# First MLP layer by seven block products instead of eight, and remainders formed by accumulating DMA

## The chip, the cores and the metric

The kernel runs on one core of a Trainium2 chip. The metric is device time in microseconds, and the time of a kernel is the median of its runs. A core has TensorE (matmuls, called PE in the profile; its weight loads are PEld), VectorE (DVE), ScalarE (ACT), GpSimd (POOL) and SyncE (SP, which issues the loads here). They run beside each other and wait for one another through semaphores. Matmuls read operands from on-chip memory and add into accumulation banks (PSUM); transfers between memories are DMAs.

## The reference

One decoder block on 512 tokens of width 1024, in float32: a gated token mixer (convolution and attention branches), and then the MLP, which is what the change touches:

```
h = rms_norm(x, g_pre_mlp) * (1 + scale2) + shift2        # 512 x 1024
y = square(relu(h @ w_mlp_in)) @ w_mlp_out                # 1024 x 4096, 4096 x 1024
x = x + gate2 * rms_norm(y, g_post_mlp)
```

## The kernel before

**Three-pass products.** TensorE multiplies in a rounded 32-bit format. To keep float32's accuracy every operand v is held as two parts, a rounded h and a remainder l = v - h, and a product is three matmuls, h·h, h·l and l·h (`mm3`, line 452). `split` (line 457) makes the parts of a block: ScalarE copies it into the rounded format, VectorE subtracts that from the original. `W` (line 470) does the same for a unit of weights, which is 128 partitions x 1024 words here; `wunit` (line 490) loads one by a 512 KB DMA on SP's queue and splits it.

**Memory.** Float data live in one arena (`f_arena`, 22400 words a partition), rounded data in another (`r_arena`, 28000 words), accumulators in eight banks. `Arena.alloc` (line 87) gives out places in program order; a buffer's place can be that of an earlier one, whose last reader is then waited for.

**Order of the work.** Every operation is recorded first (`Planner`, line 167). The planner then runs through them with a table of costs: TensorE takes its instructions in the order of the program (`key`, line 325), each other engine the ready one with the earliest due time; a DMA is ready when its buffer is free. The places are chosen again up to eight times (`PASSES`, line 47) with the times of the plan before, and the shortest plan is issued (line 385). So all instructions of the profile bear line 388, and groups are told apart by tile and shape.

**The MLP.** After normalization, transposes bring the tokens' features onto the partitions; `h2` (line 1345) holds them as 8 pairs of 128 x 512 (feature block k, all tokens), filled in two halves of 256 tokens. The 4096 hidden features are worked through in `NCH` = 4 chunks of `HPC` = 8 tiles of 128 (lines 1361 and 1362). Per chunk:

- *First layer* (from line 1526): tiles in groups of `GRP`, four at once for the first group of chunk 0 (in two halves of 256 tokens, as these come in), two at once later. Each tile is 8 feature blocks x 3 matmuls of 512 columns into a bank; ScalarE then does relu and square into `hid`.
- *Second layer* (`strassen`, line 1442): the chunk's 512 x 1024 by 1024 x 1024 product as a 2 x 2 block product with seven block products instead of eight (Strassen's scheme in Winograd's order). Sums and differences of blocks are made by VectorE on the float data and then split; `b_form` (line 1457) splits the weight blocks, two units a product, `a_form` (line 1452) the activations. A product is 2 x 4 x 3 matmuls of 512 columns. `banked` (line 1555) adds the banks to the running output and, in the last chunk, finishes the row norms and stores.

Between the layers of different chunks there is no dependence other than through buffers; `h2` stays in the rounded arena until the last chunk's first layer (line 1546).

Of the kernel before, what the change touches and what calls it, by code (L numbers as in the profile page):

```python
# [17 lines left out]
P = 128  # L18
# [374 lines left out]
def tile_hybrid_block(  # L393
# [46 lines left out]
    def emit(past, replay):  # L440
# [904 lines left out]
        h2 = []  # L1345

        def yl(t, k):
            return ra.v(mT[k][0])[:, t * P:(t + 1) * P], ra.v(mT[k][1])[:, t * P:(t + 1) * P]
# [15 lines left out]
        def hid_weights(n0, n, i0=0):  # L1364

            return {(i, kh): wunit(w_mlp_in, 4 * kh, (n0 + i) * P, 4, 256) for i in range(i0, n, 2) for kh in range(2)}

        ws0 = {(0, 0): wunit(w_mlp_in, 0, 0, 4, 256)}
        for tp in range(2):
# [25 lines left out]
            if tp == 1:  # L1395
# [4 lines left out]
            if tp == 0:  # L1400
                h2[:] = [pair(T) for _ in range(KD)]
            hsl = slice(tp * 256, (tp + 1) * 256)
            for k2 in range(KD // 2):
                b = pb.alloc()
                for q in range(2):
                    for t in range(2):
                        k = 2 * k2 + q
                        pe.transpose(pb.v(b)[:, (2 * q + t) * P:(2 * q + t + 1) * P], fa.v(xn[t])[:, k * P:(k + 1) * P], ident)
                for q in range(2):
                    k = 2 * k2 + q  # L1410
                    ps, v = pb.v(b)[:, q * 256:(q + 1) * 256], fa.alloc(256)
                    hb, lb = h2[k]
                    if k == 0:
                        act.activation(ra.v(hb)[:, hsl], ps, AF.Identity, scale=mod[:, 3, k:k + 1], bias=mod[:, 2, k:k + 1])
                        dve.tensor_scalar(fa.v(v), ps, mod[:, 3, k:k + 1], mod[:, 2, k:k + 1], ALU.mult, ALU.add)
                    else:
                        act.activation(fa.v(v), ps, AF.Identity, scale=mod[:, 3, k:k + 1], bias=mod[:, 2, k:k + 1])
                        act.copy(ra.v(hb)[:, hsl], fa.v(v))
                    dve.tensor_tensor(ra.v(lb)[:, hsl], fa.v(v), rf(hb)[:, hsl], ALU.subtract)
                    fa.free(v)  # L1420
                pb.free(b)
            fa.free(*xn)
        fa.free(G1)


        def h2s(k, a, n):
            return tuple(ra.v(b)[:, a:a + n] for b in h2[k])

        ysb = []
        G2, fin = None, []  # L1430
# [11 lines left out]
        def strassen(hv, block, banked):  # L1442
# [76 lines left out]
            banked(1, 0, ba)  # L1519
            pb.free(*ba)  # L1520

        for ch in range(NCH):
            hid = fa.alloc(HPC * T)
            hv = fa.v(hid, "p (k t) -> p k t", k=HPC)
            GRP = 4 if ch == 0 else 2
            for n0 in range(0, HPC, GRP):
                bs = [pb.alloc() for _ in range(GRP)]
                ws = ws0 if ch == 0 and n0 == 0 else hid_weights(ch * HPC + n0, GRP)
                step = 256 if ch == 0 and n0 == 0 else T
                for t0 in range(0, T, step):  # L1530
                    for i in range(GRP):
                        for k in range(KD):
                            mm3(pb.v(bs[i])[:, t0:t0 + step], ws[i - i % 2, k // 4](k % 4, (i % 2) * P, P), h2s(k, t0, step),
                                k == 0, k == KD - 1)
                for w in ws.values():
                    w.free()
                for i in range(GRP):
                    r = fa.alloc(T)
                    act.activation(fa.v(r), pb.v(bs[i]), AF.Relu)
                    act.activation(hv[:, n0 + i], fa.v(r), AF.Square)  # L1540
                    fa.free(r)
                    pb.free(bs[i])
                if ch >= NCH - 2:
                    take(late, ADAS[1])
            if ch == NCH - 1:
                for p_ in h2:
# [87 lines left out]
```

## Time and profile before

| | us |
|---|---|
| median of 3 runs | 838.59 (838.47 to 839.24) |
| profiled execution, its own time | 836.4 |
| its span, first to last instruction | 834.6 |
| TensorE busy | 808.1 |
| VectorE busy | 685.2 |
| ScalarE busy | 415.5 |
| POOL busy | 45.4 |
| DMA moved | 117.28 MB, 141 GB/s over the span |

All durations and stages come from the profiled execution. Its own time is 2.2 us below the median, and its span another 1.8 us below that. A matmul's record is longer than the distance to the next one, because matmuls overlap; a busy TensorE therefore means an occupied one, and the pace is read from starts. Idle time of an engine is given with what ended it; idle time of an engine that does not bound costs nothing.

### The profile page before, as it was taken

Reading aid. Unit: us, or ns where it says so; the run is one execution under the profiler, and the core shown is the slowest. Engines: PE = TensorE matmul, PEld = TensorE weight load, DVE = VectorE, ACT = ScalarE, POOL = GpSimd, SP = SyncE. Lnnn points to the kernel's source line nnn. Section 1 sums busy time; section 2 is a strip of 40 time slices with the busy share of each in tenths; the row PEclk is TensorE's granted clock in tenths of the full one; section 3 lists DMA queues with packets and bytes.
Section 4 is the critical chain, followed back from the end, with each engine's and each line's share of the span. In section 5 each row is a group of like instructions: output and inputs, shape, how many; then the busy total and the mean of one; then the engine's idle time right before and its main releaser. Section 6 shows DMA issues by size and latency. Waiting matters only on the chain.

```text
span 834.6 us, 10659 instructions
## 1 busy us (share of the span) xinstructions
PE 808.1 (97%) x3940; PEld 675.7 (81%) x3940; DVE 685.2 (82%) x1012; ACT 415.5 (50%) x680; POOL 45.4 (5%) x119
## 2 busy tenths in 40 slices
PE   6999999999999989999999989999999999999995
PEld 3777888899988868888888779888888888888884
DVE  4979979999999997999999779298529993975696
ACT  5463363375893346227434287375346544553641
POOL 3001040000000020000000230000000000000002
PEclk9999999999999999999999989999999999999998
DMA  9997423202353141332799650064014831660302
GB/s 310 336 311 234 148 69 98 67 27 77 101 177 102 51 128 49 101 111 91 233 353 363 210 201 27 26 202 152 0 51 132 290 132 51 197 206 1 101 1 101
DMA packets 86823, 117.28 MB, mean 141 GB/s; under 512 B 7274, under 2 KB 60627, under 8 KB 86770
## 3 DMA queue, kind: packets, MB, share of 16 engines
q1 hardware_dynamic: 86770, 116.59, 43.5%
q8 instruction: 31, 0.51, 0.2%
q14 instruction: 22, 0.18, 0.1%
HBM read 108.18 MB, written 8.39 MB: 140 GB/s over the span
## 4 chain that ended last, share of the span: by engine, by line
PE 85%; DMA 4%; DVE 3%; POOL 2%; issue 2%; ACT 2%; SPq 1%; DVEq 0%; POOLq 0%; ACTq 0%
PE psum L388 85%; DMA f_arena<-in_w_in_dram 4%; DVE f_arena L388 3%; SPq L388 1%; POOL stats L388 1%; ACT f_arena L388 1%; DMA f_arena<-in_x_dram 1%; ACT r_arena L388 1%; POOL lns L388 1%; DVE r_arena L388 0%; DVEq L1629 0%; POOLq L1629 0%; DMA rows<-in_kv_norm_g_dram 0%; DVE mod L388 0%; DVE cols L388 0%
## 5 line engine op out<-in xcount | busy, mean ns | idle before, releaser
L388 PE MATMUL psum<-r_arena 128*128 128x512 f32 (+2 forms) x3592 | 766.5, 374 | 4.0 <-ACT r_arena L388 2.5
L388 PEld LDWEIGHTS psum<-r_arena 128*128 128x128 f32 x3592 | 634.4, 190 | 121.0 <-ACT r_arena L388 3.6
L388 DVE TENSOR_TENSOR r_arena<-f_arena,r_arena 128x1024 fp32r<-128x1024 f32 (+4 forms) x232 | 247.9, 1090 | 97.1 <-PE psum L388 48.5
L388 ACT CAST r_arena<-f_arena 128x1024 fp32r<-128x1024 f32 (+4 forms) x222 | 209.7, 966 | 183.3 <-PE psum L388 111.5
L388 DVE SCALAR_TENSOR_TENSOR f_arena<-f_arena,cw 128x512 f32<-128x512 f32 x240 | 164.8, 743 | 0.0
L388 ACT ACTIVATE f_arena<-psum 128x512 f32<-128x512 f32 x64 | 38.0, 597 | 119.6 <-PE psum L388 111.3
L388 DVE TENSOR_TENSOR f_arena<-f_arena 128x1024 f32<-128x1024 f32 (+3 forms) x78 | 77.0, 1003 | 8.3 <-ACT f_arena L388 6.3
L388 ACT ACTIVATE f_arena<-f_arena 128x512 f32<-128x512 f32 (+3 forms) x100 | 58.5, 604 | 20.2 <-DVE f_arena L388 19.4
L388 DVE SCALAR_TENSOR_TENSOR f_arena<-f_arena,cT 128x256 f32<-128x256 f32 (+2 forms) x84 | 55.2, 699 | 0.1
L388 PE MATMUL psum<-ident,f_arena 128*128 128x128 f32 (+1 forms) x240 | 35.3, 288 | 11.7 <-DVE f_arena L388 7.7
L388 PEld LDWEIGHTS psum<-ident,f_arena 128*128 128x128 f32 (+1 forms) x240 | 29.2, 148 | 17.2 <-DVE f_arena L388 8.7
L388 POOL TENSOR_SCALAR stats<-stats 128x1 f32<-128x1 f32 x32 | 14.8, 463 | 467.0 <-ACT r_arena L388 361.6
L388 DVE TENSOR_TENSOR f_arena<-psum,f_arena 128x512 f32<-128x512 f32 x52 | 35.2, 684 | 4.2 <-PE psum L388 3.9
L388 ACT CAST r_arena<-psum 128x512 fp32r<-128x512 f32 (+2 forms) x57 | 30.2, 566 | 15.8 <-PE psum L388 15.4
L388 DVE TENSOR_TENSOR r_arena<-psum,r_arena 128x512 fp32r<-128x512 f32 (+2 forms) x57 | 35.7, 656 | 2.2 <-ACT r_arena L388 1.9
L388 ACT COPY f_arena<-psum 128x512 f32<-128x512 f32 (+4 forms) x42 | 19.9, 500 | 23.0 <-PE psum L388 22.7
L388 ACT ACTIVATE r_arena<-f_arena 128x512 fp32r<-128x512 f32 (+3 forms) x20 | 13.0, 648 | 21.9 <-DVE f_arena L388 18.8
L388 DVE CUSTOM_DVE_ANT_0 f_arena<-psum,mask 128x128 f32<-128x128 f32 (+3 forms) x32 | 15.0, 484 | 2.5 <-PE psum L388 2.5
L388 POOL TENSOR_SCALAR lns<-lns 128x1 f32<-128x1 f32 x4 | 5.3, 1326 | 198.5 <-ACT r_arena L388 198.5
L388 POOL TENSOR_TENSOR stats<-stats,nhalf 128x1 f32<-128x1 f32 x24 | 15.2, 633 | 1.9
L388 DVE TENSOR_SCALAR f_arena<-f_arena,stats 128x1024 f32<-128x1024 f32 x8 | 6.0, 754 | 9.9 <-POOL stats L388 9.7
L388 DVE SCALAR_TENSOR_TENSOR f_arena<-f_arena 128x512 f32<-128x512 f32 (+1 forms) x18 | 13.1, 742 | 0.0
(93 smaller groups left out, 195.4 us busy)
## 6 DMA issues: line engine op xcount, KB each, us to landing
f_arena<-in_w_ada_dram SPq DMA_DIRECT2D x16, 1024.0 KB, 5.6
f_arena<-in_w_mlp_in_dram SPq DMA_DIRECT2D x32, 512.0 KB, 5.1
f_arena<-in_w_mlp_out_dram SPq DMA_DIRECT2D x32, 512.0 KB, 5.2
f_arena<-in_w_in_dram SPq DMA_DIRECT2D x28, 512.0 KB, 4.9
f_arena<-in_x_dram SPq DMA_DIRECT2D x8, 512.0 KB, 5.3
f_arena<-in_w_ada_dram SPq DMA_DIRECT2D x16, 256.0 KB, 5.7
f_arena<-in_w_ada_dram SPq DMA_DIRECT2D x8, 512.0 KB, 6.7
h_spill<-r_arena SPq DMA_DIRECT2D x16, 256.0 KB, 5.4
```

The costliest lines, as they stand in the source:

```text
L388: getattr(self.real[o.eng], o.fn)(*o.a, **o.k)
```

## The change

**First layer.** The first group of four tiles stays as it is (`first_group`). All seven later groups of four tiles (`strassen_in`) are a 2 x 2 block product by seven block products: weight blocks of 512 features x 256 hidden (`x11` to `x22`, each one 512 KB load), token blocks of 512 features x 256 tokens. A product is 2 x 4 x 3 matmuls of 256 columns. The products are gathered in three banks; where one sum of products is read and then added to further, ScalarE copies the bank into `hid` (`keep`) and the later bank is added by VectorE, which also does relu and square there (`done`); the last quarter has relu and square on ScalarE as before.

**Tokens.** `h2` becomes four pairs of 1024 words (feature half, token half), and the float values are kept too (`h2f`). After the first group VectorE makes the four differences that the scheme needs, they are split, one of the old pairs is freed, and seven pairs of 1024 words stay until the last chunk's first layer is done.

**Remainders.** `W` gets a second way: ScalarE writes the negated value, rounded, where the remainder will be, and a DMA issued by POOL adds the float original to it in place, so -h + v is the remainder. Five of the seven weight units of each first-layer group go this way, and ten of the fourteen of each second layer; the first two products of each keep VectorE's subtraction. Activations are split as before.

```diff
-            def __init__(self, src, a, b):
+            def __init__(self, src, a, b, by_dma=False):
                 self.a, self.b = a, b
                 self.h, self.l = pair(a * b)
                 act.copy(ra.v(self.h, "p (a b) -> p a b", a=a), src)
+                if by_dma:
+                    act.mul(ra.v(self.l, "p (a b) -> p a b", a=a), src, -1.0)
+                    pool.dma_start(out=ra.v(self.l, "p (a b) -> p a b", a=a), in_=src, accum_op=ALU.add)
+                    return
...
+            for j in range(2):
+                h2[j, tp] = pair(1024)
+                h2f[j, tp] = fa.alloc(1024)
...
-            def b_form(bl):
-                return [W(fa.v(b, "p (k n) -> p k n", k=2), 2, 512) for b in bl]
+            def b_form(bl, by_dma=True):
+                return [W(fa.v(b, "p (k n) -> p k n", k=2), 2, 512, by_dma) for b in bl]
...
-            product(a11, b_form(b11), ba, True)
+            product(a11, b_form(b11, False), ba, True)
...
-            product(a12, b_form(b21), bc_, True)
+            product(a12, b_form(b21, False), bc_, True)
...
+            f = h2f
+            dve.tensor_tensor(fa.v(f[0, 0]), fa.v(f[0, 1]), fa.v(f[0, 0]), ALU.subtract)
+            dve.tensor_tensor(fa.v(f[0, 1]), fa.v(f[1, 1]), fa.v(f[0, 1]), ALU.subtract)
+            dve.tensor_tensor(fa.v(f[1, 1]), fa.v(f[1, 1]), fa.v(f[0, 0]), ALU.subtract)
+            dve.tensor_tensor(fa.v(f[1, 0]), fa.v(f[1, 0]), fa.v(f[1, 1]), ALU.subtract)
+            ra.free(*h2.pop((0, 1)))
+            for nm, b in ((2, f[1, 1]), (1, f[0, 0]), (3, f[0, 1]), (4, f[1, 0])):
+                h2[nm] = t_pair(b)
+            fa.free(*f.values())
...
+            def product(xb, y, b, first, by_dma=True):
+                w = W(fa.v(xb, "p (k n) -> p k n", k=4), 4, 256, by_dma)
+                yh, yl_ = (h2v(ra, q) for q in h2[y])
+                for m in range(2):
+                    for k in range(4):
+                        mm3(pb.v(b)[:, m * 256:(m + 1) * 256], w(k, m * P, P), (yh[:, k], yl_[:, k]), first and m == 0 and k == 0, k == 3,
+                            skip_group_check=True)
+                w.free()
...
+            def keep(i, n, b):
+                act.copy(o(i, n), ps(b))
+
+            def done(i, n, b):
+                v = o(i, n)
+                dve.tensor_tensor(v, ps(b), v, ALU.add)
+                dve.scalar_tensor_tensor(v, v, 0.0, v, op0=ALU.max, op1=ALU.mult)
+
+            x11, x12 = x(0, 0), x(0, 1)
+            ba, bb, bc_ = (pb.alloc() for _ in range(3))
+            product(x11, (0, 0), ba, True, False)
+            keep(0, 0, ba)
+            product(x12, (1, 0), bc_, True, False)
+            done(0, 0, bc_)
+            pb.free(bc_)
+            x21, x22 = x(1, 0), x(1, 1)
+            s1, s2 = fa.alloc(1024), fa.alloc(1024)
+            sub(s1, x21, x22, ALU.add)
+            sub(s2, s1, x11)
+            product(s2, 2, ba, False)
+            keep(0, 1, ba)
+            product(s1, 1, bb, True)
+            fa.free(s1)
+            keep(1, 1, bb)
+            sub(x21, x11, x21)
+            fa.free(x11)
+            product(x21, 3, ba, False)
+            fa.free(x21)
+            done(1, 1, ba)
+            sub(x12, x12, s2)
+            fa.free(s2)
+            product(x12, (1, 1), bb, False)
+            fa.free(x12)
+            done(0, 1, bb)
+            pb.free(bb)
+            product(x22, 4, ba, False)
+            fa.free(x22)
...
-            GRP = 4 if ch == 0 else 2
-            for n0 in range(0, HPC, GRP):
...
+            for n0 in range(0, HPC, 4):
+                if ch == 0 and n0 == 0:
+                    first_group(hv)
+                else:
+                    strassen_in(hv, n0, (ch * HPC + n0) * P)
```

More of the change, by code (lines that the diff above doesn't have):

```diff
@@ L1344, in emit, with h2v @@
             xr.append(b)
-        h2 = []
+        h2, h2f = {}, {}
+        def h2v(arena, b):
+            return arena.v(b, "p (k t) -> p k t", k=4)
         def yl(t, k):
@@ L1423, in emit, with h2s @@
         fa.free(G1)
-        def h2s(k, a, n):
-            return tuple(ra.v(b)[:, a:a + n] for b in h2[k])
+        def h2s(k, tp):
+            return tuple(h2v(ra, b)[:, k % 4] for b in h2[k // 4, tp])
         ysb = []
@@ L1520, in strassen, with t_pair, first_group @@
             pb.free(*ba)
+        def t_pair(b):
+            hl = pair(1024)
+            split(fa.v(b), *hl)
+            return hl
+        HG_ = 4
+        def first_group(hv):
+            bs = [pb.alloc() for _ in range(HG_)]
+            for tp in range(2):
+                for i in range(HG_):
+                    for k in range(KD):
+                        mm3(pb.v(bs[i])[:, tp * 256:(tp + 1) * 256], ws0[i - i % 2, k // 4](k % 4, (i % 2) * P, P), h2s(k, tp),
+                            k == 0, k == KD - 1)
+            for w in ws0.values():
+                w.free()
+            for i in range(HG_):
+                r = fa.alloc(T)
+                act.activation(fa.v(r), pb.v(bs[i]), AF.Relu)
+                act.activation(hv[:, i], fa.v(r), AF.Square)
+                fa.free(r)
+                pb.free(bs[i])
+            f = h2f
[7 more added lines that the diff above has]
+            fa.free(*f.values())
@@ new lines, in strassen_in, with x, sub, o @@
+        def strassen_in(hv, n0, c0):
+            def x(i, j):
+                return load(1024, w_mlp_in[512 * j:512 * j + 512, c0 + 256 * i:c0 + 256 * i + 256]
+                            .rearrange("(k p) n -> p k n", p=P), "p (k n) -> p k n", k=4)
+            def sub(o, a, b, op=ALU.subtract):
+                dve.tensor_tensor(fa.v(o), fa.v(a), fa.v(b), op)
+            def product(xb, y, b, first, by_dma=True):
[5 more added lines that the diff above has]
+                            skip_group_check=True)
+                w.free()
+            def o(i, n):
+                return hv[:, n0 + 2 * i:n0 + 2 * i + 2, 256 * n:256 * n + 256]
+            def ps(b):
+                return pb.v(b, 512, "p (m t) -> p m t", m=2)
+            def keep(i, n, b):
[33 more added lines that the diff above has]
+            fa.free(x22)
+            v = o(1, 0)
+            act.activation(v, ps(ba), AF.Relu)
+            act.activation(v, v, AF.Square)
+            pb.free(ba)
@@ L1545, in emit @@
             if ch == NCH - 1:
-                for p_ in h2:
+                for p_ in h2.values():
                     ra.free(*p_)
```

34 lines of the change are left out of this document (7 added, 27 removed).

## The prediction

> **What bounds the kernel now.** I read the page's busy shares, then the chain of waits over the last part of the run, then the engines' busy time stage by stage.
>
> ```profile
> span 834.6 us, 10659 instructions
> ...
> PE 808.1 (97%) x3940; PEld 675.7 (81%) x3940; DVE 685.2 (82%) x1012; ACT 415.5 (50%) x680; POOL 45.4 (5%) x119
> ```
>
> ```profile
> 499.93 316.33 PE psum L388 x1470
> ```
>
> The chain runs through TensorE alone from 499.9 to 816.2 us, the whole MLP. By stage (columns: stretch, length, busy time and instructions of PE, PEld, DVE, ACT, POOL; clock; DMA share; GB/s):
>
> ```profile
> core 0: us, PE busy (x) PEld busy (x) DVE busy (x) ACT busy (x) POOL busy (x), PEclk, DMA share, GB/s
> 503.00:518.60 15.60, 15.60 (x133) 15.60 (x132) 15.21 (x20) 11.62 (x23) 0.00 (x0) 1.00 0.12 35
> 518.60:540.40 21.80, 21.80 (x99) 18.04 (x98) 5.99 (x6) 7.87 (x11) 0.00 (x0) 1.00 0.09 25
> ...
> 540.40:578.50 38.10, 38.10 (x170) 31.56 (x169) 34.21 (x33) 27.09 (x32) 0.00 (x0) 1.00 0.62 193
> 578.50:622.10 43.60, 43.60 (x194) 36.13 (x193) 19.16 (x16) 16.08 (x22) 0.00 (x0) 1.00 0.05 14
> 622.10:660.30 38.20, 38.20 (x171) 31.62 (x170) 35.80 (x38) 23.58 (x24) 0.00 (x0) 1.00 0.59 187
> 660.30:703.80 43.50, 43.50 (x193) 36.04 (x192) 29.04 (x26) 15.95 (x22) 0.00 (x0) 1.00 0.37 126
> 703.80:742.00 38.20, 38.20 (x170) 31.65 (x169) 35.90 (x38) 24.07 (x25) 0.00 (x0) 1.00 0.61 193
> 742.00:785.40 43.40, 43.40 (x193) 35.94 (x192) 23.44 (x21) 19.02 (x25) 0.00 (x0) 1.00 0.17 53
> ```
>
> The stretches are: tiles 0 to 3 of the first layer (their second half), tiles 4 to 7, second layer of chunk 0, then first and second layer in turn. TensorE is never idle, so a matmul saved there is time saved, as long as its operands stay ahead. The second layers (38 us) are where others are tight: VectorE 34 to 36 us, the DMA engines 0.6. So my question is the price of a matmul, and then whether the remainders still arrive in time.
>
> **The matmuls.** One group of four tiles takes 8 x 4 x 3 = 96 matmuls of 512 columns now, and 7 products x 2 x 4 x 3 = 168 of 256 columns after. Both widths stand in the trace, dense, with the same stationary and moving buffers:
>
> ```profile
> 502.76 15.52 PE L388 MATMUL psum<-r_arena 128*128 128x256 f32 x128
> ```
>
> ```profile
> 519.76 260.60 PE L388 MATMUL psum<-r_arena 128*128 128x512 f32 x1149
> ```
>
> ```profile
> L388 PE MATMUL psum<-r_arena 128*128 128x256 f32 x128 | 15.5, 283 | 0.0
> ```
>
> ```profile
> L388 PE MATMUL psum<-r_arena 128*128 128x512 f32 x1344 | 305.0, 389 | 0.0
> ```
>
> A record is longer than the pace, since matmuls overlap; first start to last start is the piece less one record. So the pace is (15.52 - 0.28)/127 = 120.0 ns at 256 columns and (260.60 - 0.39)/1148 = 226.7 ns at 512: half the width costs more than half. A group goes from 96 x 226.7 = 21.76 to 168 x 120.0 = 20.16 us, 1.60 us less (7%, not the eighth of the arithmetic). Seven groups: **-11.2 us**.
>
> The Trainium skill's page "TensorE: Matmul & The Clock Gate" (Back-to-back issue gap) gives N/2.4 + 2.5 ns for a single stream, 109.2 and 215.8 ns here. By that a group would save 2.37 us and the seven 16.6 us. Both rows of this trace are 11 ns above it, and the row decides.
>
> **The element work.**
>
> ```profile
> L388 DVE TENSOR_TENSOR r_arena<-f_arena,r_arena 128x1024 fp32r<-128x1024 f32 x106 | 126.8, 1219 | 74.1 <-PE psum L388 46.7 <-issue 17.2 <-ACT r_arena L388 8.3
> L388 ACT CAST r_arena<-f_arena 128x1024 fp32r<-128x1024 f32 x105 | 108.2, 1053 | 66.0 <-PE psum L388 40.7 <-issue 11.2 <-DMA f_arena<-in_w_mlp_out_dram 6.0
> L388 DVE TENSOR_TENSOR f_arena<-f_arena 128x1024 f32<-128x1024 f32 x42 | 50.5, 1220 | 6.6 <-ACT f_arena L388 6.3
> L388 DVE TENSOR_TENSOR f_arena<-psum,f_arena 128x512 f32<-128x512 f32 x49 | 33.2, 685 | 4.2 <-PE psum L388 3.9
> L388 ACT ACTIVATE f_arena<-f_arena 128x512 f32<-128x512 f32 x29 | 18.3, 632 | 0.8
> L388 ACT ACTIVATE f_arena<-psum 128x512 f32<-128x512 f32 x29 | 17.3, 598 | 71.7 <-PE psum L388 71.6
> ...
> L388 ACT COPY f_arena<-psum 128x512 f32<-128x512 f32 x8 | 4.6, 579 | 1.9 <-PE psum L388 1.9
> ```
>
> ```profile
> L388 ACT ACTIVATE r_arena<-f_arena 128x1024 fp32r<-128x1024 f32 x4 | 4.2, 1056 | 2.8 <-DMA f_arena<-in_x_dram 2.8
> ```
>
> VectorE, per first-layer group: four splits (4.9 us) become two splits, four block sums and three times an addition out of PSUM plus a relu-square (about 0.69 each): 2.4 + 4.9 + 4.1 = 11.4, so +6.5, +13 a chunk. The second layer loses ten splits, -12.2. A chunk's total stays near 65 us (29.0 + 35.9 in chunk 2) of 79; it moves out of the tight stage. ScalarE, per group: four copies and four relu-squares (4.2 + 4.9) become seven copies, five negations at 1.06, three copies out of PSUM at 0.58 and one relu-square: 15.7, so +6.6. The second layer gains ten negations, 10.6: 34 us of 38, and 37.7 of 38.1 in chunk 0. All of it lies beside TensorE; I cost it at nothing, but ScalarE now has no room left in the second layer. The four sums and four splits of the tokens after the first group (9.8 us of VectorE) fall into 518.6 to 540.4, where it had 6.0 busy of 21.8; without that room the second product would wait, 0 to 3 us; I take 0. The float copies of the tokens, held until then, take 4096 words from loads: 0 to 2 us, I take 0, as that stretch moves 25 to 35 GB/s.
>
> **The accumulating transfers.** No such transfer, and none issued from POOL, is in the trace. There are 75: ten in each second layer, five in each group. The 512 KB neighbours, issue to landing:
>
> ```profile
> f_arena<-in_w_mlp_out_dram SPq DMA_DIRECT2D x32, 512.0 KB, 5.2
> ...
> f_arena<-in_w_attn_out_dram SPq DMA_DIRECT2D x8, 512.0 KB, 3.6
> ...
> x_spill<-f_arena SPq DMA_DIRECT2D x4, 512.0 KB, 3.2
> ```
>
> Second layers move 193 GB/s at a share of 0.62, so 311 GB/s when busy: 1.7 us for 512 KB. An accumulate reads its destination too. Call L the time from the end of the negation to the landing. Low end 3.2 (nothing added, nothing queued); high end 5.2 + 1.7 = 6.9 (second pass, among the loads). I take the unqueued load and a second pass, **L = 3.6 + 1.7 = 5.3 us**. 75 x 1.7 us more engine time would be hidden if it came in time.
>
> The Trainium skill's page "Collectives: The Full Stack" (The bandwidth ceiling) says a reducing transfer emits two reads for one write and so runs at half rate: no run shows it yet, and by it the second pass is real. Its page "DMA: Bandwidth & Descriptors" (Anatomy of one DMA) fits 2.0 us + bytes/436 GB/s, which for 1 MB read makes an estimated L of 4.4, and by the condition below no stall.
>
> **Where L decides.** The arena of rounded values (28000 words) holds 27 buffers of 1024. Tokens took 16 x 512 words, 8 of them, leaving 19. After, seven pairs of 1024 stay until the last chunk's first layer, leaving 13. A second-layer product reads six (two weight pairs, one of activations) for 24 x 226.7 = 5.44 us: three products fitted, now two and a spare. The casts that wait for TensorE above (40.7 us in all) show that buffers already gate the splits. So product p+2 is formed while p+1 runs. Count from the end of p: its first weight pair comes free at -1.36 (last read at 18 of 24 matmuls), the rest at 0. With the spare used for the next copy, ScalarE negates until -0.31, copies the second unit until 0.74, negates until 1.80; its transfer lands at 1.80 + L and is needed 1.36 after product p+2 starts. The step T from product to product is at least L + 0.44; if the spare is not there, one copy later, L + 1.5. At L = 5.3 T is 5.74, 0.30 over 5.44. Products 3 to 7 use transfers in chunks 0, 1 and 2 (the last chunk has the arena back): 15 x 0.30 = **+4.4 us**. Behind a waiting TensorE stands everything; ScalarE's next copy waits for the same buffers. On POOL a transfer that waits for its negation holds up only later transfers and, in the last chunk, the row norms. On SP a load waits until the old buffer is read, now by the landing, 1.1 + L - 1.2 = 5 us later than by the split. That is covered: the loads for the second layer that begins at 622.1 are issued 49 us ahead,
>
> ```profile
> L388 SPq DMA_DIRECT2D f_arena<-in_w_mlp_out_dram x8: 367/368/368, 558.0 to 572.9; - x8
> ```
>
> and a load that came 5 us late without this cover would cost up to 5 us of idle TensorE. In the first layer a product reads two buffers for 2.9 us, so a remainder has some 14 us, against 2.1 + L: no stall.
>
> **Sum.** The profiled execution took 836.4 us, 834.6 of it the span: 836.4 - 11.2 + 4.4 = 829.6. The median is 2.2 above it (838.59), so 831.8, **832 us**.
>
> **Rivals.**
> - *The buffer ring decides: slower.* Place: products 3 to 7 of the second layers of chunks 0 to 2. The 11.2 us are gone at 0.75 us a product: L = 5.75 with the spare, 4.7 without. For it: the loads land at 5.2 without any second pass, and the DMA share there is already 0.6. Against: 3.6 and 3.2 when unqueued, and loads may shift to the first layers, at 0.05 to 0.37. At L = 5.3 without the spare 15 x 1.35 = 20 us, 848; at 6.9 with it 15 x 1.9 = 28 us, 856.
> - *Nothing to measure.* The same ring at 0.6 to 0.85 us a product, 837 to 840.
> - *The DMA engines fill up: slower.* A chunk's loads are 0.59 x 38.2 + 0.05 x 43.6 = 25 us of engine time. Twenty accumulates at 1.7 or 3.4 us add 34 or 67, against 78.5 us. Only at the high end (92) do they bind, by 13 us a chunk, some 870 us.
> - *The full gain.* If 256 columns cost half of 512 (113.4 ns) in the new groups, each saves 21.76 - 19.05 = 2.7 us, all seven 19 us, and with no stall the time is 820. The dense row at 120.0 ns, with the same operands, speaks against it. The formula of the Trainium skill's page "TensorE: Matmul & The Clock Gate" (Back-to-back issue gap) would give 822.
>
> **How the numbers follow.** A change within 0.2% (1.7 us) can't be told from none. Forecast (no stall to 0.55 us a product; 827 to 836) 0.47, full gain 0.03, no change 0.08, ring 0.36, engines full 0.06. So faster 0.50, same 0.08, slower 0.42. The range from 827 to 852 holds the forecast, no change, and three quarters of the ring's cases (0.27): 0.82. The forecast's own range is 827 to 836.
>
> **What would show it.** 256-column matmuls of the first layers at 120 ns from start to start, 20.2 us a group; TensorE gaps, if any, inside the second layers' products 3 to 7, released by transfers from POOL into the rounded arena, none in the last chunk; the transfers' landing near 5.3 us; VectorE near 24 us and ScalarE near 34 in second layers. The forecast is wrong if the landing is over 5.7 us, if gaps stand in first layers, or if the DMA share stays near 1 for a whole chunk.

## The result

The changed kernel took 880.66 us (879.21 to 883.5, 4 runs) beside 838.80 us (838.47 to 839.24) for the kernel before: a ratio of 1.0503, 95% interval [1.0474, 1.0532]. It is 5% slower; the forecast of 832 us was wrong in sign, and the time lies beyond the range.

The page of the changed kernel (`q0` is the queue of the transfers that POOL issues; the last column of a DMA issue is the median time from issue to landing):

```profile
span 881.7 us, 12016 instructions
...
PE 814.2 (92%) x4444; PEld 696.1 (79%) x4444; DVE 691.5 (78%) x1036; ACT 495.8 (56%) x759; POOL 112.5 (13%) x194
...
DMA  9997233104450412236994564999399974999992
...
q0 software_dynamic: 10800, 39.33, 23.1%
...
r_arena<-f_arena POOLq DMA_DIRECT2D x75, 512.0 KB, 9.1
...
f_arena<-in_w_mlp_in_dram SPq DMA_DIRECT2D x32, 512.0 KB, 9.4
f_arena<-in_w_mlp_out_dram SPq DMA_DIRECT2D x32, 512.0 KB, 12.7
```

The same two rows of the kernel before, whose loads of the second layer landed in 5.2 us:

```profile
DMA  9997423202353141332799650064014831660302
...
f_arena<-in_w_mlp_in_dram SPq DMA_DIRECT2D x32, 512.0 KB, 5.1
```

TensorE has 504 more, narrower matmuls and nearly the same busy time. What changed is the row of the DMA engines: before, it rose to 6 tenths (once 8) around the second layers and fell to nothing between them; now most of the last 18 slices are 9s. The median load of the MLP's weights takes about twice as long to land. The price of one accumulating transfer can be read here: 23.1% of 881.7 us is 203.7 us of all 16 engines, over 75 transfers **2.72 us each**. On their own queue, from POOL's issue:

```profile
DMA to landing us min/median/max: 4.6/9.1/13.3
```

By stage (columns as in the prediction's stages; the DMA share is the second number from the end):

```profile
540.00:580.00 40.00, 32.49 (x135) 24.45 (x133) 24.13 (x23) 32.07 (x37) 8.94 (x11) 1.00 0.89 198
580.00:620.00 40.00, 39.05 (x289) 37.62 (x290) 20.87 (x23) 26.71 (x32) 8.50 (x10) 0.96 1.02 249
620.00:660.00 40.00, 33.44 (x172) 28.26 (x170) 28.92 (x30) 23.67 (x26) 5.80 (x7) 0.96 0.60 131
660.00:700.00 40.00, 34.76 (x205) 30.11 (x206) 25.18 (x26) 26.07 (x29) 8.50 (x11) 0.96 1.05 251
700.00:740.00 40.00, 33.67 (x239) 32.08 (x238) 23.82 (x27) 19.81 (x24) 4.24 (x6) 0.91 0.61 164
740.00:780.00 40.00, 34.59 (x152) 26.42 (x151) 24.18 (x26) 27.19 (x28) 9.37 (x11) 1.00 1.03 248
780.00:820.00 40.00, 34.40 (x268) 33.92 (x267) 22.76 (x24) 26.04 (x31) 7.00 (x8) 0.91 1.00 249
```

The engines are full in long stretches, at 249 GB/s, where the kernel before moved 311 GB/s when busy. TensorE, which never paused in these layers before, has holes in each of these stretches. Who ended the waits, from the first group to the end (us in total, times, longest):

```profile
PE psum L388 <- DMA r_arena<-f_arena: 21.6, 18, 3.0
...
PE psum L388 <- DVE f_arena L388: 13.7, 5, 6.3
...
PE psum L388 <- ACT f_arena L388: 5.4, 1, 5.4
```

```profile
DVE f_arena L388 <- DMA f_arena<-in_w_mlp_in_dram: 37.7, 6, 12.9
...
DVE f_arena L388 <- DMA f_arena<-in_w_mlp_out_dram: 13.2, 2, 8.4
```

```profile
SPq L388 <- DMA r_arena<-f_arena: 256.6, 38, 32.1
```

```profile
L388 PE MATMUL psum<-r_arena 128*128 128x512 f32 x672 | 162.4, 397 | 23.4 <-DMA r_arena<-f_arena 20.9 <-DVE f_arena L388 2.2
```

So there are two roads to the loss, short and long by the number of steps, not by the time that they cost. One is short: TensorE waits for a remainder, nearly always (20.9 of 21.6 us) ahead of a matmul of 512 columns, which is the second layer. The other is longer: a weight load lands late, VectorE, which takes its work in order, stands at the block sum that needs it, and the additions behind it that free the banks or give TensorE its operands are late too. The row of SP's queue shows what ties the roads together: SP's loads now wait for transfers to let go of the float buffers. One case of the long road, in order of time:

```profile
697.80 23.56 PE L388 MATMUL psum<-r_arena 128*128 128x256 f32 x195
...
722.27 2.48 DVE L388 TENSOR_TENSOR f_arena<-f_arena 128x1024 f32<-128x1024 f32 x2 [8.35 <-DMA f_arena<-in_w_mlp_out_dram]
...
727.69 2.72 PE L388 MATMUL psum<-r_arena 128*128 128x256 f32 x11 [6.33 <-DVE f_arena L388]
```

VectorE idles 8.35 us for a load of the *second* layer, in the middle of a *first* layer, and TensorE then idles 6.33 us for VectorE. The first row also settles the pace: (23.56 - 0.28)/194 = 120.0 ns, as read from the kernel before. The last row shows that a pause costs more than it lasts: its matmuls are some (2.72 - 0.28)/10 = 240 ns apart, half the pace, and the granted clock from 727.6 to 730.0 us was 0.50.

### The profile page after: what moved, and what is told of

The parts are those of the page before. It is cut to its first block, busy times and chain, and to the rows that moved or that the text cites. A ratio compares the mean times of both kernels' runs of the same rounds, so it can differ in the third digit from the quotient of the medians.

```text
span 881.7 us, 12016 instructions
## 1 busy us (share of the span) xinstructions
PE 814.2 (92%) x4444; PEld 696.1 (79%) x4444; DVE 691.5 (78%) x1036; ACT 495.8 (56%) x759; POOL 112.5 (13%) x194
## 3 DMA queue, kind: packets, MB, share of 16 engines
q0 software_dynamic: 10800, 39.33, 23.1%
## 5 line engine op out<-in xcount | busy, mean ns | idle before, releaser
L388 PE MATMUL psum<-r_arena 128*128 128x512 f32 (+3 forms) x4096 | 771.8, 349 | 43.5 <-DMA r_arena<-f_arena 21.6
L388 PEld LDWEIGHTS psum<-r_arena 128*128 128x128 f32 x4096 | 654.6, 193 | 146.1 <-DMA r_arena<-f_arena 31.2
L388 ACT CAST r_arena<-f_arena 128x1024 fp32r<-128x1024 f32 (+4 forms) x247 | 234.4, 971 | 190.4 <-PE psum L388 113.0
L388 DVE TENSOR_TENSOR r_arena<-f_arena,r_arena 128x1024 fp32r<-128x1024 f32 (+4 forms) x182 | 189.7, 1058 | 36.4 <-ACT r_arena L388 22.1
L388 DVE TENSOR_TENSOR f_arena<-f_arena 128x1024 f32<-128x1024 f32 (+3 forms) x110 | 115.4, 1068 | 58.0 <-DMA f_arena<-in_w_mlp_in_dram 37.7
L388 ACT ACTIVATE r_arena<-f_arena 128x1024 fp32r<-128x1024 f32 (+3 forms) x95 | 91.1, 972 | 39.8 <-DVE f_arena L388 18.7
L388 POOL DMA_DIRECT2D r_arena<-f_arena x75 | 65.7, 875 | 287.8 <-ACT r_arena L388 251.5
L388 DVE TENSOR_TENSOR f_arena<-psum,f_arena 128x512 f32<-128x512 f32 x73 | 49.2, 686 | 48.3 <-PE psum L388 42.1
L388 ACT ACTIVATE f_arena<-f_arena 128x384 f32<-128x384 f32 (+3 forms) x79 | 45.2, 599 | 15.0 <-DVE f_arena L388 14.7
L388 PE MATMUL psum<-ident,f_arena 128*128 128x128 f32 (+1 forms) x240 | 35.5, 291 | 12.7 <-DVE f_arena L388 8.7
L388 DVE SCALAR_TENSOR_TENSOR f_arena<-f_arena 128x512 f32<-128x512 f32 (+1 forms) x39 | 27.6, 713 | 0.2
## 6 DMA issues: line engine op xcount, KB each, us to landing
f_arena<-in_w_mlp_out_dram SPq DMA_DIRECT2D x32, 512.0 KB, 12.7
```

The lines of the kernel that those rows point to most:

```text
L388: getattr(self.real[o.eng], o.fn)(*o.a, **o.k)
```

## The experiments

### What each part is worth

The expectations use short names. Theory A: the transfers fill the DMA engines. Rival B: thirteen rounded buffers are too few. Rival C: the block products of the first layer themselves cost the time. Rival D: ScalarE is full in the second layers.

*no_add* leaves the accumulating transfers out:

```diff
-                    pool.dma_start(out=ra.v(self.l, ...), in_=src, accum_op=ALU.add)
```

> The changed kernel without the accumulating DMAs: the negated rounded value stays where the remainder would be, so the remainders of 75 weight units are left out; ScalarE's negations, the buffers and all else stay. Theory A: 828 to 832 us. Rival D (ScalarE is full in second layers, 34 to 38 of 38 us): 840 or more with TensorE released by ScalarE. Rival B: no effect of the number of buffers is left without the latency, so also 828 to 832.

Measured: 823.23 us, ratio 0.9834 [0.9815, 0.9853], beside 836.81 for the kernel before, measured with it. The two stages that were tightest, and TensorE's last matmuls here, in the kernel before and in the changed one:

```profile
540.00:579.00 39.00, 39.00 (x190) 32.97 (x189) 32.06 (x31) 36.35 (x42) 0.00 (x0) 1.00 0.48 149
...
622.00:661.00 39.00, 39.00 (x204) 33.58 (x203) 35.45 (x38) 35.57 (x38) 0.00 (x0) 1.00 0.58 190
```

```profile
799.62 11.72 PE L388 MATMUL psum<-r_arena 128*128 128x512 f32 x51
```

```profile
798.64 25.77 PE L388 MATMUL psum<-r_arena 128*128 128x512 f32 x113
```

```profile
856.20 15.04 PE L388 MATMUL psum<-r_arena 128*128 128x512 f32 x65 [1.12 <-DMA r_arena<-f_arena]
```

The last matmul ends at 811.3 us without the transfers, 824.4 before and 871.2 with them. Without them TensorE is dense, with ScalarE 36 us busy of 39. So Strassen's first layer, the copies, the negations and the smaller ring together, with 75 remainders left out, are worth -13.6 us, and the 75 transfers alone cost 880.7 - 823.2 = 57 us. Most of the 13.6 is the matmuls': from the last transposes to the start of the last second layer the kernel before takes 786.12 - 502.56 = 283.6 us and *no_add* 773.06 - 501.43 = 271.6, 12 less. Another 1.1 us lies ahead of that, where the granted clock (485 to 500 us) was 0.77 before and 1.00 here.

Up to the last matmul the transfers cost 871.2 - 811.3 = 60 us, and TensorE's own rows take these apart. From 500 us on, its matmuls of 256 and 512 columns have 17.8 + 23.4 = 41 us of pauses in the changed kernel and none in *no_add*, and they are busy for 167.8 + 162.4 = 330 us instead of 157.7 + 153.1 = 311. Much of these 19 us can be the clock: by its column in the stages above, at most 40 x (3 x 0.04 + 2 x 0.09) = 12 us, an estimate that takes TensorE as busy in all of the slow time. The rest of the 19 was not taken apart.

*all_vector* keeps the new first layer and lets VectorE form all remainders:

```diff
-                if by_dma:
+                if False:
```

> The changed kernel, but every remainder is subtracted by VectorE; no accumulating DMA and no negation is left. Theory A (75 accumulating transfers at 2.7 us of all sixteen DMA engines fill these): the loss goes, 828 to 834 us, landing of loads back near 5 us. Rival B (thirteen rounded buffers are too few, whoever forms the remainder): 840 us or more, gaps of TensorE in second layers. Rival C (the block products of the first layer themselves: bank waits, VectorE's sums): stays over 850, gaps in first layers.

849.26 us, ratio 1.0147 [1.0126, 1.0168]. From 480 us on TensorE pauses for 16.7 us, 12.8 of them for VectorE and none for a transfer: the loss here is mainly VectorE's.

```profile
PE 805.4 (95%) x4444; PEld 692.1 (82%) x4444; DVE 773.5 (91%) x1111; ACT 426.8 (50%) x684; POOL 50.6 (6%) x119
```

VectorE gained 88 us over the 685.2 before. The change needs some relief of VectorE; what it used for it is the question.

*before_13_buffers* takes the ring by itself, in the kernel before:

```diff
+        held = [ra.alloc(1024) for _ in range(6)]     # freed with h2
```

> The kernel before, with six buffers of 1024 rounded words held back from the start of the MLP until the last chunk's first layer is done, so 13 instead of 19 are free. Rival B: second layers stall, 841 us or more. Theory A: within 2 us of 838.8, since VectorE's subtraction needs no more lead than two products.

838.42 us, 1.0012 [0.9996, 1.0028]: by itself, with VectorE forming the remainders, the smaller ring costs nothing that can be measured.

*before_dma_second* puts the 40 transfers of the second layers into the kernel before, with its 19 buffers and its old first layer; *dma_first_layer* and *dma_second_layer* keep 35 or 40 of the 75 transfers of the changed kernel:

```diff
-            def b_form(bl, by_dma=True):                   # dma_first_layer
+            def b_form(bl, by_dma=False):
...
-            def product(xb, y, b, first, by_dma=True):     # dma_second_layer
+            def product(xb, y, b, first, by_dma=False):
```

> The kernel before with only the second part of the change: ten remainders of each second layer by accumulating DMA, 40 in all; first layer in eight products, nineteen buffers. Theory A: within 3 us of before, landing 5 to 6 us, no gaps. Rival B with nineteen buffers: the same; so gaps here would say that the transfers hurt beside the loads even with buffers to spare.

> The changed kernel with the accumulating DMAs in the first layers only (35; five of seven units a group); second layers subtract on VectorE. Theory A (engine time: loads 25 us and 10 x 2.72 us a chunk, 52 of 78.5): no stall by DMA, VectorE in second layers as in the kernel before; 12 to 8 us faster than before. If any accumulating DMA beside the loads costs TensorE time, whatever the total, slower than before.

> The changed kernel with the accumulating DMAs in the second layers only (40; ten a chunk); first layers subtract on VectorE. Theory A by the total alone (25 + 27 of 78.5 us): 10 to 5 us faster than before. Rival B (thirteen buffers leave a remainder less than two products, and the landing is 4.6 us even alone): gaps in products 3 to 7 of the second layers, 3 us faster to 12 us slower than before.

847.46 us, 1.0109 [1.0086, 1.0132]; 863.2, 1.0295 [1.0267, 1.0323]; 865.1, 1.0302 [1.0269, 1.0335]. By the total of engine time the first should have been within 3 us of the kernel before and the other two faster than it; none is, so the total by itself does not give the time. The first of them has neither the new first layer nor the small ring, and loses 9 us all the same. Its waits and landings:

```profile
PE psum L388 <- DMA r_arena<-f_arena: 6.8, 9, 1.5
```

```profile
r_arena<-f_arena POOLq DMA_DIRECT2D x40, 512.0 KB, 10.1
f_arena<-in_w_mlp_in_dram SPq DMA_DIRECT2D x32, 512.0 KB, 10.4
f_arena<-in_w_mlp_out_dram SPq DMA_DIRECT2D x32, 512.0 KB, 10.0
```

### Which property of the transfers

Two theories were left: a remainder that takes a fixed, long way to land (few buffers, held float originals, a plan that thinks the transfer cheap), or engine time. *plain_copy* keeps queue, waits and bytes written, and drops the addition, and with it the rounding of what is written (`rf` is the float view); *half_width* adds half the columns; *dma_half* sends 41 units, spread over both layers, and lets VectorE do the rest:

```diff
-  pool.dma_start(out=ra.v(self.l, ...), in_=src, accum_op=ALU.add)
+  pool.dma_start(out=rf(self.l, ...), in_=src)                                       # plain_copy
...
+  pool.dma_start(out=ra.v(self.l)[:, :512], in_=(...)[:, :512], accum_op=ALU.add)    # half_width
...
-                return [W(fa.v(b, ...), 2, 512, by_dma) for b in bl]                 # dma_half
+                return [W(fa.v(b, ...), 2, 512, by_dma and u == 1) for u, b in enumerate(bl)]
...
-            product(s2, 2, ba, False)                      # and likewise product(x12, (1, 1), ...)
+            product(s2, 2, ba, False, False)
```

> The changed kernel with POOL's 75 accumulating DMAs made plain copies of the same size between the same buffers (the remainder is then the value itself, so the remainders are not computed). Theory A with the second read as the price: a transfer's engine time falls from 2.7 to about 1.7 us, in all by 75 us of engine time, the time goes to 835 to 850. If the price were POOL's way of issuing, engine time and time stay at 2.7 and about 880 us.

> The changed kernel with each of the 75 accumulating DMAs over the first 512 of its 1024 columns only (the other half of these remainders is left as the negated rounded value). Theory A (engine time): 1.4 us a transfer instead of 2.7, the engine time of a plain copy, so near the plain copy's result, 832 to 842 us. If the price lay in the number of accumulating transfers, their issue on POOL or their fixed latency: over 855.

> The changed kernel with about half of the accumulating DMAs: three of seven units a group in the first layers (21), every second unit of products 3 to 7 in the second layers (20). Theory A: engine time 25 + 11 x 2.72 = 55 of 78.5 us a chunk and VectorE near 76; 12 to 6 us faster than before, landing 5 to 6 us. Rival B: some gaps in second layers, 5 us faster to 3 us slower.

836.02 us, 0.9995 [0.9976, 1.0014]; 839.9, 1.0028 [1.0014, 1.0043]; 840.99, 1.0032 [1.002, 1.0044]. The copy's queue:

```profile
q0 software_dynamic: 10800, 39.33, 12.0%
...
r_arena<-f_arena POOLq DMA_DIRECT2D x75, 512.0 KB, 5.6
```

12.0% of its 835.4 us is 100.2 us, 1.34 us each: same bytes, same packets, half the engine time. The addition, with the rounding, doubles a transfer (2.03 times); no run has one without the other. POOL's issue of a copy also took less, 0.54 instead of 0.87 us. Half the width takes 13.7% of 838.2 us, 114.8 us, and 41 transfers take 13.5% of 838.1 us, 113.1 us. Three quite different edits that each bring the engine time to 100 to 115 us land within 5 us of one another, 13 to 18 us above *no_add*; at 204 us the price is 57. Between these runs it grows faster than the engine time (*dma_first_layer* and *dma_second_layer*, at 95 and 112 us, lie higher; more on them below). In these three the road is the short one, TensorE's waits for remainders (*plain_copy*, *half_width*, *dma_half*):

```profile
PE psum L388 <- DMA r_arena<-f_arena: 7.7, 6, 2.6
```

```profile
PE psum L388 <- DMA r_arena<-f_arena: 11.4, 10, 3.7
```

```profile
PE psum L388 <- DMA r_arena<-f_arena: 9.8, 10, 2.3
```

VectorE ended only 1.6, 0.9 and 2.0 us of pauses there. All of the waits for transfers stand in the second layers of chunks 0 to 2 and none in the last chunk's, which is the place that the prediction gave for a ring of buffers that is too small.

The other explanations: *source_rounded* adds from the rounded copy, so that the float buffer is free at once; *planned_double* lets the planner count twice the bytes for an accumulating transfer; *pool_subtract* has POOL subtract instead:

```diff
+  pool.dma_start(out=ra.v(self.l, ...), in_=rf(self.h, ...), accum_op=ALU.add)       # source_rounded
...
-            o.dma = b                                                                # planned_double
+            o.dma = 2 * b if "accum_op" in k else b
...
+  pool.tensor_tensor(ra.v(self.l, ...), src, rf(self.h, ...), ALU.subtract)          # pool_subtract
```

> The changed kernel, all 75 accumulating DMAs kept, but each adds the rounded copy instead of the float original, so the remainders of these units come out as zero. Size, engines and count are the same; only the float buffer no longer has the transfer as its last reader, so that the loads into it need not wait for the landing. If the held float buffers are most of the loss: 835 to 850 us. If the engines' time alone is: 870 to 885.

> The changed kernel, same work, with the planner counting twice the bytes for an accumulating DMA, so that order and buffers are chosen for its measured 2.7 us. If the loss came from an order planned for transfers that land too late (VectorE blocked in order behind sums of late loads): 845 to 865 us. If the engines are simply full: 870 to 885.

> The changed kernel with the 75 remainders subtracted by POOL as a compute engine, no negation and no accumulating DMA. If POOL and VectorE do not hinder each other: 823 to 832 us, faster than both kernels. If their subtractions shut each other out: VectorE's mean over 1.3 us and 840 us or more.

880.93 us, 1.0517 [1.0492, 1.0541]; 886.67, 1.0577 [1.0535, 1.0619]; 913.51, 1.09 [1.0875, 1.0925]. In the first, SP waits for none of these transfers any more, but the MLP's loads still land in 11.4 and 16.6 us and TensorE waits 29.8 us for remainders: the held float buffers alone are not the cause. Counting the transfers double in the plan did not help either. The third loses in another way:

```profile
L388 POOL TENSOR_TENSOR r_arena<-f_arena,r_arena 128x1024 fp32r<-128x1024 f32 x75 | 224.9, 3020 | 166.5 <-PE psum L388 102.2 <-ACT r_arena L388 62.8 <-issue 1.5
L388 DVE TENSOR_TENSOR f_arena<-f_arena 128x1024 f32<-128x1024 f32 x77 | 153.9, 2021 | 2.0 <-DMA f_arena<-in_w_mlp_in_dram 1.5
...
L388 DVE TENSOR_TENSOR f_arena<-psum,f_arena 128x512 f32<-128x512 f32 x71 | 47.3, 679 | 4.0 <-PE psum L388 3.9
```

VectorE's block sums went from 1220 to 2021 ns, while its additions out of PSUM stayed at 679. The Trainium skill's page "SBUF — State Buffer" (Who interferes with whom) says that a VectorE instruction with two inputs in that memory contends with a GpSimd instruction that reads it; the rows agree, with those numbers.

### Which road: the remainders or the loads

*add_to_scratch* lets the 75 transfers add into two scratch buffers that no matmul reads:

```diff
-                    pool.dma_start(out=ra.v(self.l, ...), in_=src, accum_op=ALU.add)
+                    scr.append(scr.pop(0))
+                    pool.dma_start(out=ra.v(scr[0], ...), in_=src, accum_op=ALU.add)
```

> The changed kernel with all 75 accumulating DMAs kept, of the same size and from the same float buffers, but adding into two scratch buffers that no matmul reads; the remainders of these units are left as the negated rounded value. TensorE waits for no transfer any more; the loads still share the engines with them. If the loss is the wait for the remainders themselves: 825 to 832 us. If the transfers do their harm by delaying the loads: 850 us or more, with VectorE and TensorE waiting for late loads.

882.43 us, 1.0541 [1.0515, 1.0567]. TensorE waits for no transfer, and nearly all of the loss is there; the last row is its last matmuls, which end at 866.4 us:

```profile
DVE f_arena L388 <- DMA f_arena<-in_w_mlp_in_dram: 42.4, 4, 14.3
...
PE psum L388 <- DVE f_arena L388: 23.4, 4, 7.4
PE psum L388 <- DVE r_arena L388: 18.7, 3, 8.8
```

```profile
828.14 38.29 PE L388 MATMUL psum<-r_arena 128*128 128x512 f32 x168
```

But these transfers still hold the float buffers, and the two scratch buffers put them in a line: SP's loads wait 284.0 us for transfers, and then land in 6.1 and 7.7 us. *add_uncoupled* drops that tie: the transfers read a weight in DRAM, and only a one-column read on POOL orders them behind the negation.

```diff
+                    scr.append(scr.pop(0))
+                    pool.tensor_scalar(seen, rf(self.l)[:, 0:1], 1.0, None, ALU.mult)
+                    pool.dma_start(out=ra.v(scr[0]), in_=w_mlp_out[0:P, :], accum_op=ALU.add)
```

> The changed kernel with all 75 accumulating transfers, but each reads 512 KB of a weight from DRAM and adds it to one of two scratch buffers that no matmul reads; it only starts once the negated value is there (a read of one column on GpSimd). So no matmul and no buffer of a load waits for a transfer; the remainders are the negated rounded values, the second read is left out. If the loss needs a wait on the transfers (TensorE, or the buffers that they hold), the loads come late by little and the time is 825 to 835, near the 823 without any transfer. If the engine time of the transfers alone makes the loads late, the time is 850 or more, VectorE waits for the MLP's weight loads and TensorE for VectorE.

869.04 us, 1.0365 [1.0329, 1.0402]. No row of TensorE's or SP's waits names a transfer of POOL's, and yet:

```profile
f_arena<-in_w_mlp_in_dram SPq DMA_DIRECT2D x32, 512.0 KB, 15.6
f_arena<-in_w_mlp_out_dram SPq DMA_DIRECT2D x32, 512.0 KB, 12.4
```

```profile
DVE f_arena L388 <- DMA f_arena<-in_w_mlp_in_dram: 33.2, 6, 7.5
...
PE psum L388 <- DVE f_arena L388: 15.9, 7, 7.1
```

```profile
807.12 38.29 PE L388 MATMUL psum<-r_arena 128*128 128x512 f32 x168
```

The last matmul ends at 845.4 us. Counted from the 811.3 of *no_add*, the engine time alone (24.4% of 867.8 us, 211.7 us) costs 34 us of the 60 that the changed kernel loses up to its last matmul: 16.0 + 7.3 = 23 us of pauses, and 11 us of longer matmuls. The rest of this run's time is of its own making: after the last matmul the row norms on POOL stand behind the backlog of transfers, and VectorE waits 12.9 us for them. Rounded buffers are still tied, as the one-column read comes late on POOL (ScalarE waits 12.2 us for it), which itself waits 113.3 us for the two scratch buffers. So the 34 us are an upper estimate for engine time alone, and for transfers that read DRAM. By difference the remaining 26 us go with the ties of the transfers to TensorE and to the float buffers, and no run splits them cleanly: *source_rounded*, which cuts the second, gave nothing back, and *add_to_scratch*, which cuts the first and adds a line of its own, 5 us up to the last matmul (871.2 to 866.4).

### A lighter share

Four kernels looked for a share that pays: *half_relu_scalar* and *first_relu_scalar* are *dma_half* and *dma_first_layer* with relu and square of the sums on ScalarE; *spread_relu_scalar* has 36 transfers, four a group and two a second layer; *first_21* has three a group and none in second layers, both with that move.

```diff
-                dve.scalar_tensor_tensor(v, v, 0.0, v, op0=ALU.max, op1=ALU.mult)
+                act.activation(v, v, AF.Relu)
+                act.activation(v, v, AF.Square)
```

> The version with about half of the accumulating DMAs (41), with the relu and square of the first layers' sums moved from VectorE to ScalarE (4 us of VectorE a chunk less). If VectorE's load is what is left in that version: 830 to 836. If the waits for transfers in second layers are: 838 to 842, as without the move.

> The version with accumulating DMAs in the first layers only (35, 863 us), with the same move of relu and square to ScalarE. If its loss is a VectorE with no room (77 of 78.5 us a chunk by the rows) that stops behind late loads: 840 to 852. If the loss is the transfers' engine time alone: 858 to 866.

> As the half version with relu and square on ScalarE, but 36 transfers, four of seven units a group in the first layers, where a remainder has some 14 us, and two a chunk in second layers. If the wait of the second layers is what is left: 828 to 835 us, faster than both kernels. If transfers at any place delay the loads: 840 or more.

> Three accumulating transfers in each of the seven groups of the first layers (21 in all), none in the second layers; there VectorE subtracts, and ScalarE does the relu and the square of the sums. By the loads on a chunk of 78 us: DMA engines some 25 + 6 x 2.7 = 41 us, so loads land near 6 us; VectorE some 89 - 1.2 x 6 - 4 = 78 us, all of the chunk. If a full VectorE costs what it cost with all subtractions on it, less the eased part, 838 to 846. If only the DMA engines' load counts, 825 to 835.

846.91 us, 1.011 [1.0072, 1.0149]; 862.86, 1.0306 [1.028, 1.0331]; 851.23, 1.0159 [1.0135, 1.0183]; 840.16, 1.0036 [1.0017, 1.0055]. Easing VectorE gained nothing where transfers are many. With 21 transfers the DMA share is no longer full, and VectorE is, in the second layers; TensorE still pauses, in the first layers above all (39.53 of 43 us below):

```profile
622.00:661.00 39.00, 39.00 (x202) 33.46 (x201) 37.10 (x39) 23.10 (x25) 2.62 (x3) 1.00 0.50 142
661.00:704.00 43.00, 39.53 (x300) 38.52 (x298) 34.06 (x34) 28.87 (x39) 2.61 (x3) 0.96 0.65 178
```

No version that computes all of it beat the kernel before. One thing is settled only in part. *dma_first_layer*, *dma_second_layer* and *dma_half* have nearly equal engine time (11.0% of 860.4 us is 94.6 us; 13.0% of 863.3 us is 112.2; 113.1), and the first two are 22 and 24 us slower than the third. They put the same work into half the stages; *dma_first_layer* and then *dma_half*:

```profile
580.00:620.00 40.00, 40.00 (x302) 38.83 (x301) 23.09 (x27) 26.32 (x32) 6.95 (x8) 0.94 0.91 223
620.00:660.00 40.00, 40.00 (x201) 34.04 (x200) 38.83 (x39) 23.68 (x26) 0.87 (x1) 1.00 0.23 70
```

```profile
580.00:620.00 40.00, 40.00 (x331) 39.83 (x331) 27.71 (x31) 23.88 (x30) 4.35 (x5) 1.00 0.68 169
620.00:660.00 40.00, 36.94 (x162) 29.75 (x161) 36.02 (x37) 27.26 (x29) 5.22 (x6) 1.00 0.67 171
```

That a crowded stage (0.91, then 0.23) is what costs, rather than the even 0.68 and 0.67, fits, but *dma_first_layer* also leaves all of the second layer's subtractions to VectorE (38.83 of 40). Two runs hold that fixed: *first_relu_scalar* and *first_21* both leave these subtractions to VectorE and differ only in 14 remainders of the first layers, formed by a transfer or by VectorE. The first takes 862.86 us, the second 840.16, and TensorE's pauses ahead of 256 columns fall from 22.7 to 7.1 us. So a VectorE that is full in the second layers does not by itself make the 22 us; six transfers in a chunk's first layer instead of ten win back as much. Whether it is their crowding or their total stays open, as both differ, and for *dma_second_layer* there is no such pair.

## Why the prediction was wrong

- **The matmuls: right.** -11.2 us was the sum; *no_add* gave -13.6 with dense TensorE, 12 of them over the stretch of these matmuls; the pace was 120.0 ns as read. The full-gain rival, 19 us by the matmuls, fell with it.
- **Element work at no cost: right where it could be seen.** In *no_add* VectorE and ScalarE lie beside a dense TensorE, ScalarE about as full as forecast. The relief of VectorE in the second layers is not there, though: the prediction named 24 us, and *no_add* still has 32.06 and 35.45 of 39; why was not looked into. The cover is real but thin: with all subtractions on VectorE, in *all_vector*, it is gone, at 849.
- **The step that failed: "75 x 1.7 us more engine time would be hidden if it came in time."** The accumulate costs 2.72 us, not 1.7, which is inside the 1.7 to 3.4 that the rival of full engines allowed. By that rival's own terms a chunk then needs 25 + 20 x 2.72 = 79.4 us of the engines in 78.5, and the new first layers shorten a chunk by two groups' gain, to 75.3. The text said that only the high end binds; the bound lies at (78.5 - 25)/20 = 2.7 us, in the middle of its range. I gave it 0.06.
- **And it was priced wrongly.** The rival charged the excess of demand over time. But waits begin well before the engines are full: *plain_copy*, with 25 + 20 x 1.34 = 52 us of a chunk, already pays 13 us of the 13.6, and *dma_half* with its 113 us pays 18. What comes late there are the remainders of the second layers.
- **L = 5.3 us was near the fastest transfer and wrong for this kernel.** The lowest landing is 4.6 us from POOL's issue; the median is 9.1, over the 5.7 that the prediction named as the point where it falls. I derived L from unqueued neighbours while adding the queue myself. So the stall in second layers, +4.4 us in the sum (15 x 0.30 is 4.5), measured 20.9. The Trainium skill's page "Collectives: The Full Stack" (The bandwidth ceiling), by which a reducing transfer reads twice and runs at half rate, was the better guide to the engine time: 2.72 over 1.34 us agrees with it. The 4.4 us estimated from the Trainium skill's page "DMA: Bandwidth & Descriptors" (Anatomy of one DMA) is near the 4.6 and says nothing of a queue.
- **"That is covered" failed for the same reason.** "In the first layer ... no stall" held for the remainders, for which matmuls of 256 columns waited 0.7 us; but they waited 11.5 us for VectorE and 5.4 for ScalarE. A late load was priced at up to 5 us of TensorE and taken as covered by 49 us; loads landed in 9.4 and 12.7 us, their issue waited for transfers, and VectorE, in order, carried the delay across stages.
- **The ring rival (0.36): right in its place, short in its price.** The waits that it foretold, on transfers in second layers, are there: 20.9 us ahead of 512-column matmuls, near its 20 to 28, and nearly all of the pauses in the three lighter kernels. But they are about half of the pauses in the changed kernel, and *add_to_scratch* lost as much without them. Its cause is open: a ring of thirteen costs nothing without the transfers (1.0012), and 40 transfers lose 9 us with nineteen; no run has the new first layer with a larger ring.

## What to carry to other kernels

Before moving work from a compute engine to a DMA, add up the DMA engines' time stage by stage as for any other engine, count an accumulate that rounds at twice a plain copy, as measured here, and compare the sum with the shortened stage. In this kernel, where the second layers stood at 0.6, with 100 us more of engine time the remainders that TensorE needs next came late; with 204 us the loads did as well, and an in-order engine that waited for one passed the delay on to work that needed no load at all. A landing time read from unqueued neighbours was a lower bound.

## What the runs showed of the hardware

- An accumulating 512 KB transfer within on-chip memory took 2.72 us of all engines, a plain one, which does not round, 1.34, a 256 KB accumulate 114.8/75 = 1.53: more than half, with the same 10800 packets.
- Issuing such a transfer kept POOL busy for 875 ns on average, 65.7 us for all 75.
- A subtraction of 128 x 1024 on POOL took 3.02 us, and VectorE's two-input work beside it 1.66 times its time (2021 over 1220 ns).
- The granted clock was 0.91 to 0.96 over five of the seven 40 us stretches shown, in all of which TensorE paused, and 0.50 right behind the pause of 6.33 us; in *no_add*, without pauses, it was 1.00 from 500 to 800 us. By these figures its share of the 60 is estimated at no more than some 12 us in these stretches.
